# Operand tiles of the matrix products at different byte offsets within their buffers

## The chip, the cores and the metric

The kernel runs on one core of a Trainium2 chip, as one launch. The metric is the device time of that launch in microseconds (us). The kernel before was run three times: 972.31, 972.32 and 972.38 us, median 972.32 us. One further execution was taken by the hardware profiler.

## The reference

A trunk of two layers on 256 tokens of width 1024. Each layer is a half-step SwiGLU feed-forward block (FFN), a mixing block (two kinds of attention and a causal pooling, run side by side on one projected input), and a second half-step FFN. Every block starts with an RMS norm, and one more norm ends the trunk. All is float32.

```python
for l in range(2):
    x = x + 0.5 * swiglu(rmsnorm(x, ffn1_norm[l]), ffn1_w_gu[l], ffn1_w_down[l])
    x = x + hybrid_mixing(rmsnorm(x, mix_norm[l]), w_in[l], ..., w_out[l], pos)
    x = x + 0.5 * swiglu(rmsnorm(x, ffn2_norm[l]), ffn2_w_gu[l], ffn2_w_down[l])
return rmsnorm(x, final_norm)

def swiglu(h, w_gu, w_down):          # 1024 -> 2 x 2816 -> 1024
    gu = h @ w_gu
    g, u = gu[..., :D_FF], gu[..., D_FF:]
    return (jax.nn.silu(g) * u) @ w_down
```

## The kernel before

**Split products.** Nearly all products are made of three matmuls on the type float32r. Each operand is kept as a rounded part (high) and the rest that the rounding left (low), and high x high, high x low and low x high are added up in PSUM. The activations lie transposed, features on partitions and 256 tokens in a row. `mmw` (lines 229 to 231) loads a 128 x 128 piece of a weight as the stationary operand and streams 256 tokens past it. `mm3` (lines 222 to 224) has it the other way round: tokens are stationary and 288 to 512 columns of a weight stream.

**Tiles that the products read.**
- `hT` holds the normed input of a block, 8 chunks of 128 features, each with 256 high and 256 low values: 16 KB in each partition, one buffer for the whole kernel. Lines 403 and 410 write it; the gate and up products of an FFN (`gu_tile`) and the projections of the mixing block (`chunks`, `mix_head`) read it.
- `ph` and `pl` are the high and low parts of an FFN's inner activation, 1 KB in each partition, in 8 buffers each that are used in turn (`ptile`, line 524). The down product (`down`) reads them. In the mixing block the same buffers hold the inputs of the output projection.
- `hi` and `lo` are the high and low parts of a weight, 4 KB in each partition, in 8 buffers each. A weight arrives by DMA in `raw` (4 buffers, line 299), ScalarE rounds it to `hi` (line 320), and VectorE subtracts to get `lo` (line 335).

In the kernel before every one of these tiles starts at a multiple of 64 bytes. Counted within blocks of 128 bytes, `hT` starts at 64, and `ph`, `pl`, `hi` and `lo` start at 0. The norms are numbered: 0 and 3 feed the first FFN of a layer, 1 and 4 its mixing block, 2 and 5 its second FFN.

**Order.** An FFN goes over 22 chunks of 128 inner features. A chunk takes two gate/up tiles of 8 x 3 matmuls on `hT`, and, two chunks later, its down product, 8 x 3 matmuls on `ph` and `pl` into four PSUM banks. The kernel writes the order of the work on TensorE, ScalarE, VectorE and the DMA queue by hand, from an event simulation with fixed costs (`Issue`). These costs know nothing of addresses.

**Test products.** After all else, lines 1186 to 1195 issue 24 matmuls into a PSUM bank that nobody reads: 6 each on `hT` (512 columns), on a bfloat16 copy `pb` of part of `x`, on zeros `pz`, and on two halves of `hT`. GpSimd makes `pb` and `pz` at the start of the kernel (lines 1170 to 1174).

Of the kernel before, what the change touches and what calls it, by code (L numbers as in the profile page):

```python
# [10 lines left out]
F32 = mybir.dt.float32  # L11
F32R = mybir.dt.float32r
I32 = mybir.dt.int32
AF = mybir.ActivationFunctionType
ALU = mybir.AluOpType

P = 128
D = 1024
KC = 8
# [15 lines left out]
GUARD = 0.7  # L35
WB = 8
RB = 4

C_MASK, C_T, C_ROPE, C_INV, C_AB, C_END = 0, 256, 512, 640, 1152, 1164
V_B, V_PS, V_G, V_END = 0, 12, 16, 16 + L * 384  # L40
# [144 lines left out]
def trunk(ctx: ExitStack, tc: tile.TileContext, wpk, xin, gains, cst, vec, fst, out):  # L185
    nc = tc.nc
    V, A, T = nc.vector, nc.scalar, nc.tensor
    q = Issue()
    LAT = q.LAT

    cp = ctx.enter_context(tc.tile_pool(name="cp", bufs=1))
# [35 lines left out]
    def mmw(o, hi, lo, xh, xl, start, stop):  # L227

        T.matmul(o, lhsT=hi, rhs=xh, start=start, stop=False, skip_group_check=True)  # L229
        T.matmul(o, lhsT=hi, rhs=xl, start=False, stop=False, skip_group_check=True)  # L230
        T.matmul(o, lhsT=lo, rhs=xh, start=False, stop=stop, skip_group_check=True)  # L231
        return q.on("PE", 3 * 256 / 2185.0)
# [19 lines left out]
    vm = cp.tile([P, 2, 384], F32, name="vm")  # L252
    vf = cp.tile([P, 2, 384], F32, name="vf")
    up = [cp.tile([P, 272], F32, name=f"up{i}") for i in range(2)]
    hT = cp.tile([P, KC, 2, 256], F32R, name="hT")
    hTh, hTl = hT[:, :, 0, :], hT[:, :, 1, :]
    mhalf = cp.tile([P, 2], F32, name="mhalf")
    one = cp.tile([P, 1], F32, name="one")
    lf = [cp.tile([P, P], F32, name=f"lf{i}") for i in range(2)]
# [14 lines left out]
    def tbs(tb):  # L274
        return slice(tb * P, (tb + 1) * P)
# [32 lines left out]
    def hi_task():  # L308
        for u in range(NU):
            yield ev_slot[u], R_PREP  # L310
            rk = R_CHAIN + 0.1 * u if u < PARTS0 else R_PREP
            yield ev_raw[u], rk
            if u >= PARTS0:
                yield from calm("ACT", rk)
            w, r = units[u][3], raws[u]
            if units[u][0] == "poolw":
                h = wp.tile([P, 1024], F32, tag="hi", bufs=WB, name=f"hi{u}")
            else:
                h = wp.tile([P, 1024], F32R, tag="hi", bufs=WB, name=f"hi{u}")
            A.copy(h[:, :w], r[:, :w])  # L320
            his[u] = h
            ev_hi[u].set(act(w) + LAT)

    def lo_task():
        for u in range(NU):
            rk = R_CHAIN + 0.1 * u if u < PARTS0 else R_PREP
            yield ev_hi[u], rk, "DVE"
            if u >= PARTS0:
                yield from calm("DVE", rk)
            w, r, h = units[u][3], raws[u], his[u]  # L330
            if units[u][0] == "poolw":
                t = ev_hi[u].t
            else:
                lo = wp.tile([P, 1024], F32R, tag="lo", bufs=WB, name=f"lo{u}")
                V.tensor_tensor(out=lo[:, :w], in0=r[:, :w], in1=h[:, :w].bitcast(F32), op=ALU.subtract)  # L335
                los[u] = lo
                t = dve(w)
            ev_raw_free[u + RB].set(t + LAT)
            ev_w[u].set(t + LAT)

    uses = {}

# [26 lines left out]
    class N:  # L369


        def __init__(self, gi):
            self.gi = gi
            self.ev_h = [Ev() for _ in range(KC)]
            self.ss = sp.tile([P, 512], F32, tag="ss", bufs=1, name="ss")
            self.ev_ss = Ev()
            self.n = 0
            self.r, self.ev_r = None, Ev()
            self.R, self.Rh, self.ev_R = None, None, Ev()

    def resid(nm, i, acc, ev_acc, Rh):

        rk = R_CHAIN + 0.1 * i
        xs = x[:, 2 * i:2 * i + 2, :]
        yield ev_acc, rk, "DVE"
        if acc is not None:
            a = acc.rearrange("p (k t) -> p k t", k=2)
            if Rh is not None:
                d = sp.tile([P, 2, 256], F32, tag="dx", bufs=3, name="dx")
                V.tensor_tensor(out=d, in0=a, in1=bc(Rh, 2), op=ALU.mult)  # L390
                q.give(acc, dve(512) + LAT)
                V.tensor_tensor(out=xs, in0=xs, in1=d, op=ALU.add)  # L392
                t = dve(512)
            else:
                V.tensor_tensor(out=xs, in0=a, in1=xs, op=ALU.add)
                t = dve(512)
                q.give(acc, t + LAT)
            yield t + LAT, rk, "ACT"
        if nm is None:
            return  # L400
        for k in (2 * i, 2 * i + 1):
            g = fs[:, X_G + KC * nm.gi + k:X_G + KC * nm.gi + k + 1]
            A.activation(hTh[:, k, :], x[:, k, :], AF.Copy, scale=g)  # L403
            t = act(256)
            q.spawn(resid_lo(nm, k, g, t + LAT, rk))
        q.spawn(square(nm, i, xs, t + LAT))

    def resid_lo(nm, k, g, t, rk):
        yield t, rk, "DVE"
        V.scalar_tensor_tensor(out=hTl[:, k, :], in0=x[:, k, :], scalar=g, in1=hTh[:, k, :].bitcast(F32),  # L410
                               op0=ALU.mult, op1=ALU.subtract)
        nm.ev_h[k].set(dve(256) + LAT)

# [107 lines left out]
            nc.sync.dma_start(out[tb, :, c], h)  # L521


    def ptile(nm):
        return sp.tile([P, 256], F32R, tag=nm, bufs=8, name=nm)

    class F:

# [14 lines left out]
    def gu_tile(g, fc, j, k, b):  # L543
        n = parts(g.l, g.f, fc)
        m = KC // n
        u = g.W("gu", (fc, k // m))
        c = slice((k % m) * 256 + j * P, (k % m) * 256 + j * P + P)
        t = mmw(b[:, 0:256], his[u][:, c], los[u][:, c], hTh[:, k, :], hTl[:, k, :], k == 0, k == KC - 1)
        if k % m == m - 1:
            done(u, t, 2)  # L550
        return t
# [146 lines left out]
    def mix_head(g, tb):  # L698

        yield Banks(2), R_HEAD + 0.1 * tb  # L700
        bA, bB = q.take(2)
        for k in range(KC):
            yield g.nm.ev_h[k], R_HEAD + 0.1 * tb
            u = pos[("bq", g.l, k)]
            yield ev_w[u], R_HEAD + 0.1 * tb
            lh, ll, wh, wl = hTh[:, k, tbs(tb)], hTl[:, k, tbs(tb)], his[u], los[u]
            mm3(bA[:, 0:384], lh, ll, wh[:, 422:806], wl[:, 422:806], k == 0, k == KC - 1)
            t = mm3(bB[:, 0:422], lh, ll, wh[:, 0:422], wl[:, 0:422], k == 0, k == KC - 1)
            done(u, t, 2)
            yield t, R_HEAD + 0.1 * tb  # L710
        q.spawn(lowrank(g, tb, bA, t))
        q.spawn(gates(g, tb, bB, t))
        if tb == 1:
            q.spawn(chunks(g))
            q.spawn(qkv(g))
            q.spawn(decay(g))
            q.spawn(mix_out(g))
            for n, (kind, j) in enumerate(ATT_ORDER):
                q.spawn(attn(g, n, kind, j))
# [173 lines left out]
    def chunks(g):  # L893

        for kind in CHUNKS:
            yield Banks(1), R_MAIN
            b, = q.take(1)
            u = pos[(kind, g.l, 0)]
            yield ev_w[u], R_MAIN
            for k in range(KC):  # L900
                c = slice(k * P, (k + 1) * P)
                t = mmw(b[:, 0:256], his[u][:, c], los[u][:, c], hTh[:, k, :], hTl[:, k, :], k == 0, k == KC - 1)
                yield t, R_MAIN
            done(u, t)
            if kind[0] == "f":
                q.spawn(fox_evac(g, int(kind[3]), b, t))
            else:
                q.spawn(pool(g, int(kind[4]), b, t))
# [238 lines left out]
    with tc.manual_schedule(engines={mybir.EngineType.PE, mybir.EngineType.Activation, mybir.EngineType.DVE, mybir.EngineType.SP}):  # L1147
# [12 lines left out]
            nc.gpsimd.memset(up[i][:, 0:16], 0.0)  # L1160
            nc.gpsimd.memset(lf[i], 0.0)

        pb = cp.tile([P, 512], mybir.dt.bfloat16, name="pb")
        pz = cp.tile([P, 512], F32R, name="pz")

        def rest():
            yield 60.0, R_LATE
            dma(C_END / 2, lambda: nc.sync.dma_start(cs, cst))
            dma(V_END / 2, lambda: nc.sync.dma_start(ve, vec))
            nc.gpsimd.tensor_copy(pb, x[:, 0:2, :].rearrange("p k t -> p (k t)"))  # L1170
            zz = sp.tile([P, 256], F32, tag="pc", bufs=1, name="zz")
            nc.gpsimd.memset(zz, 0.0)
            nc.gpsimd.tensor_copy(pz[:, 0:256], zz)
            nc.gpsimd.tensor_copy(pz[:, 256:512], zz)

        q.spawn(rest())
        q.spawn(load_task())
# [4 lines left out]
            q.spawn(resid(n0, i, None, ev_x[i], None))  # L1182
        q.spawn(ffn(F(0, 0, n0), after_ffn1(0)))
        q.run()

        b, = q.take(1)
        w = hT[:, 0, 0, 0:P]
        for n in range(6):
            T.matmul(b, lhsT=hT[:, n, 0, 0:P], rhs=hT[:, n, :, :].rearrange("p a t -> p (a t)"), start=n == 0, stop=n == 5)
        for n in range(6):  # L1190
            T.matmul(b, lhsT=pb[:, 0:P], rhs=pb, start=n == 0, stop=n == 5)
        for n in range(6):
            T.matmul(b, lhsT=pz[:, 0:P], rhs=pz, start=n == 0, stop=n == 5)
        for n in range(6):
            T.matmul(b[:, 0:256], lhsT=hT[:, n, 0, 0:P], rhs=hT[:, n, :, 0:P], start=n == 0, stop=n == 5)

# [99 lines left out]
```

## Time and profile before

| | |
|---|---|
| median of 3 runs | 972.32 us |
| profiled execution | 973.32 us |
| its span, first to last instruction | 971.5 us |
| granted TensorE clock, mean | 0.996 of full speed |
| TensorE busy, matmul (PE) / weight load (PEld) | 952.3 / 927.7 us |
| VectorE (DVE) / ScalarE (ACT) / GpSimd (POOL) busy | 625.3 / 501.5 / 58.2 us |
| moved by DMA | 168.92 MB, mean 174 GB/s |

The matmul records overlap: one of 256 columns is recorded as some 280 ns long, while the next starts 113 to 119 ns after it. So busy time says nothing of TensorE's speed; the distance from start to start does, and it is read here from rows of the timeline.

### The profile page before, as it was taken

The numbers are of one execution on the slowest core, as the hardware profiler recorded it, in microseconds if no ns is written. First come the engines' busy times: TensorE is split into PE (matmuls) and PEld (weight loads), VectorE is DVE, ScalarE is ACT, GpSimd is POOL, SyncE is SP. The second block draws the span as 40 slices with busy tenths as digits, with TensorE's granted clock in tenths as the row PEclk, the third lists the DMA queues.
The fourth block names the chain that finished last, engine by engine and source line by source line (L and its number), as shares of the span: only waits on it lengthen the run. The fifth ranks groups of instructions, "written<-read, shape, count | busy, mean of one in ns | idle before, by whom it ended". The sixth has DMA issues, their size and how long they took to land.

```text
span 971.5 us, 18312 instructions
## 1 busy us (share of the span) xinstructions
PE 952.3 (98%) x7547; PEld 927.7 (95%) x7548; DVE 625.3 (64%) x1018; ACT 501.5 (52%) x797; POOL 58.2 (6%) x108
## 2 busy tenths in 40 slices
PE   8999999998999999999999999999999999999999
PEld 7999999997999999999999999999989999999997
DVE  6755555568996755555585555556599766555553
ACT  6544444456664644444464444445466665444442
POOL 1000000022220000000000000000504000000000
PEclk8999999999999999999999999999999999999999
DMA  7775555522453766655547655653423647566631
GB/s 247 233 265 189 185 186 191 161 84 93 136 192 103 263 199 195 188 187 188 177 137 232 194 181 189 182 180 104 149 91 117 211 134 263 189 196 194 191 115 44
DMA packets 48324, 168.92 MB, mean 174 GB/s; under 512 B 5360, under 2 KB 5744, under 8 KB 48240
## 3 DMA queue, kind: packets, MB, share of 16 engines
q1 hardware_dynamic: 48096, 167.66, 53.7%
q8 instruction: 59, 0.97, 0.4%
q14 instruction: 25, 0.20, 0.1%
q10 hardware_dynamic: 144, 0.09, 0.0%
HBM read 166.68 MB, written 1.05 MB: 173 GB/s over the span
## 4 chain that ended last, share of the span: by engine, by line
PE 85%; DVE 10%; POOL 2%; issue 1%; ACT 1%; DMA 1%; SPq 0%; DVEq 0%; POOLq 0%
PE bank L230 24%; PE bank L229 24%; PE bank L231 24%; PE bank L224 3%; PE bank L223 3%; PE bank L222 3%; DVE lo L335 3%; DVE fqk L944 1%; DVE pl L987 1%; PE bank L235 1%; POOL rsn L356 1%; PE bank L239 1%; DMA x<-xin 1%; DVE sm L998 1%; DVE e L1013 1%
## 5 line engine op out<-in xcount | busy, mean ns | idle before, releaser
L335 DVE TENSOR_TENSOR lo<-raw,hi 128x1024 fp32r<-128x1024 f32 (+3 forms) x320 | 382.7, 1204 | 187.4 <-ACT hi L320 184.6
L229 PE MATMUL bank<-hT,hi 128*128 128x256 f32 x1536 | 433.5, 282 | 0.0
L231 PE MATMUL bank<-hT,lo 128*128 128x256 f32 x1536 | 429.5, 280 | 0.6 <-DVE lo L335 0.4
L230 PE MATMUL bank<-hT,hi 128*128 128x256 f32 x1536 | 429.2, 279 | 0.0
L320 ACT CAST hi<-raw 128x1024 fp32r<-128x1024 f32 (+3 forms) x320 | 328.1, 1029 | 171.9 <-PE bank L230 111.6
L229 PEld LDWEIGHTS bank<-hT,hi 128*128 128x128 f32 x1536 | 291.7, 190 | 1.0
L231 PEld LDWEIGHTS bank<-hT,lo 128*128 128x128 f32 x1536 | 290.1, 189 | 1.3 <-DVE lo L335 1.1
L230 PEld LDWEIGHTS bank<-hT,hi 128*128 128x128 f32 x1536 | 289.6, 189 | 1.1
L229 PE MATMUL bank<-ph,hi 128*128 128x256 f32 x656 | 186.1, 284 | 0.0
L230 PE MATMUL bank<-pl,hi 128*128 128x256 f32 x656 | 184.8, 282 | 0.8 <-DVE pl L365 0.8
L231 PE MATMUL bank<-ph,lo 128*128 128x256 f32 x656 | 184.8, 282 | 0.0
L230 PEld LDWEIGHTS bank<-pl,hi 128*128 128x128 f32 x656 | 123.5, 188 | 1.1 <-DVE pl L365 1.0
L229 PEld LDWEIGHTS bank<-ph,hi 128*128 128x128 f32 x656 | 123.6, 188 | 0.1
L231 PEld LDWEIGHTS bank<-ph,lo 128*128 128x128 f32 x656 | 123.5, 188 | 0.0
L580 ACT ACTIVATE s<-s 128x256 f32<-128x256 f32 x88 | 36.4, 418 | 154.0 <-DVE s L576 153.9
L576 DVE TENSOR_TENSOR s<-bank,R 128x256 f32<-128x256 f32 x88 | 37.1, 424 | 43.2 <-PE bank L231 40.1
L365 DVE TENSOR_TENSOR pl<-p,ph 128x256 fp32r<-128x256 f32 x88 | 37.1, 424 | 38.0 <-ACT ph L362 38.0
L362 ACT CAST ph<-p 128x256 fp32r<-128x256 f32 x88 | 35.5, 406 | 25.3 <-DVE p L590 25.2
L356 POOL TENSOR_TENSOR rsn<-m,mhalf 128x2 f32<-128x2 f32 x6 | 9.3, 1551 | 647.2 <-DVE m L448 647.2
L590 DVE TENSOR_TENSOR p<-bank,s 128x256 f32<-128x256 f32 x88 | 36.6, 418 | 12.1 <-PE bank L231 9.6
L403 ACT ACTIVATE hT<-x,fs 128x256 fp32r<-128x256 f32 x48 | 21.8, 502 | 32.2 <-DVE x L392 18.3
L222 PE MATMUL bank<-lo,ph 128*128 128x512 f32 x88 | 34.7, 394 | 0.0
(155 smaller groups left out, 730.5 us busy)
## 6 DMA issues: line engine op xcount, KB each, us to landing
raw<-wpk SPq DMA_DIRECT2D x294, 512.0 KB, 4.1
raw<-wpk SPq DMA_DIRECT2D x16, 403.0 KB, 3.2
raw<-wpk SPq DMA_DIRECT2D x4, 288.0 KB, 3.5
x<-xin SPq DMA_DIRECT2D x4, 256.0 KB, 5.7
raw<-wpk SPq DMA_DIRECT2D x4, 256.0 KB, 5.7
out<-h SPq DMA_DIRECT2D x4, 256.0 KB, 2.1
raw<-wpk SPq DMA_DIRECT2D x2, 384.0 KB, 3.2
cs<-cst SPq DMA_DIRECT2D x1, 582.0 KB, 5.9
```

What stands on the lines that cost most here:

```text
L222: T.matmul(o, lhsT=lh, rhs=rl, start=start, stop=False)
L223: T.matmul(o, lhsT=ll, rhs=rh, start=False, stop=False)
L229: T.matmul(o, lhsT=hi, rhs=xh, start=start, stop=False, skip_group_check=True)
L230: T.matmul(o, lhsT=hi, rhs=xl, start=False, stop=False, skip_group_check=True)
L231: T.matmul(o, lhsT=lo, rhs=xh, start=False, stop=stop, skip_group_check=True)
L320: A.copy(h[:, :w], r[:, :w])
L335: V.tensor_tensor(out=lo[:, :w], in0=r[:, :w], in1=h[:, :w].bitcast(F32), op=ALU.subtract)
L362: A.copy(dh, src)
L365: V.tensor_tensor(out=dl, in0=src, in1=dh.bitcast(F32), op=ALU.subtract)
L576: V.tensor_tensor(out=s, in0=b[:, 0:256], in1=g.nm.R, op=ALU.mult)
L580: A.activation(s, s, AF.Silu)
L590: V.tensor_tensor(out=p, in0=b[:, 0:256], in1=g.s[fc], op=ALU.mult)
```

## The change

Each of the tiles gets some room in its buffer, and starts at an offset into it. The offset of `hT` goes by norm (64, 0, 32, 0, 0 and 16 bytes for the norms 0 to 5). Those of `ph` and `pl` go by turns, 0, 64, 32, 16, 96, 8, 80 and 4 bytes, in buffers whose pitch grows from 1024 to 1120 bytes. `hi` and `lo` get 0 bytes four times and 64 bytes four times in turn, and their pitch grows from 4096 to 4160 bytes. Counted within blocks of 128 bytes, the operands of the 6576 matmuls of 256 columns then start so:

| operand | before | after |
|---|---|---|
| `hT`, norms 0 to 5 | 64 | 0, 64, 96, 64, 64, 80 |
| `ph`, `pl` | 0 | spread over the block; in 1488 of 1968 matmuls at a multiple of 16 bytes, in 480 of them 4 or 8 bytes past one |
| `hi`, `lo` | 0 | 0 or 64 |
| `hT` less weight | 64 in all 4608 | 64 in 984, 0 in 1512, neither (16, 32, 80, 96) in 2112 |

The test products go, and with them `pb` and `pz`. No other instruction is added, removed or moved: the rows on each of the five engines are the same in the same order.

```diff
+OFF_X = [16, 0, 8, 0, 0, 4]
+OFF_P = [0, 16, 8, 4, 24, 2, 20, 1]
+OFF_W = [0, 0, 0, 0, 16, 16, 16, 16]
...
-    hT = cp.tile([P, KC, 2, 256], F32R, name="hT")
-    hTh, hTl = hT[:, :, 0, :], hT[:, :, 1, :]
+    hT = cp.tile([P, KC * 512 + 32], F32R, name="hT")
...
-                h = wp.tile([P, 1024], F32R, tag="hi", bufs=WB, name=f"hi{u}")
+                h = place(F32R, "hi", u)
...
-                lo = wp.tile([P, 1024], F32R, tag="lo", bufs=WB, name=f"lo{u}")
+                lo = place(F32R, "lo", u)
...
+    def place(dt, nm, u):
+        o = turn(nm, OFF_W)
+        return wp.tile([P, 1040], dt, tag=nm, bufs=WB, name=f"{nm}{u}")[:, o:o + 1024]
...
+            o = OFF_X[gi]
+            v = hT[:, o:o + KC * 512].rearrange("p (k s t) -> p k s t", k=KC, s=2)
+            self.hh, self.hl = v[:, :, 0, :], v[:, :, 1, :]
...
+    count = {"ph": 0, "pl": 0, "hi": 0, "lo": 0}
+
+    def turn(nm, offs):
+
+        count[nm] += 1
+        return offs[(count[nm] - 1) % len(offs)]
+
     def ptile(nm):
-        return sp.tile([P, 256], F32R, tag=nm, bufs=8, name=nm)
+        o = turn(nm, OFF_P)
+        return sp.tile([P, 280], F32R, tag=nm, bufs=8, name=nm)[:, o:o + 256]
...
-            nc.gpsimd.tensor_copy(pb, x[:, 0:2, :].rearrange("p k t -> p (k t)"))
-            zz = sp.tile([P, 256], F32, tag="pc", bufs=1, name="zz")
-            nc.gpsimd.memset(zz, 0.0)
-            nc.gpsimd.tensor_copy(pz[:, 0:256], zz)
-            nc.gpsimd.tensor_copy(pz[:, 256:512], zz)
...
-        b, = q.take(1)
-        w = hT[:, 0, 0, 0:P]
-        for n in range(6):
-            T.matmul(b, lhsT=hT[:, n, 0, 0:P], rhs=hT[:, n, :, :].rearrange("p a t -> p (a t)"), start=n == 0, stop=n == 5)
-        for n in range(6):
-            T.matmul(b, lhsT=pb[:, 0:P], rhs=pb, start=n == 0, stop=n == 5)
-        for n in range(6):
-            T.matmul(b, lhsT=pz[:, 0:P], rhs=pz, start=n == 0, stop=n == 5)
-        for n in range(6):
-            T.matmul(b[:, 0:256], lhsT=hT[:, n, 0, 0:P], rhs=hT[:, n, :, 0:P], start=n == 0, stop=n == 5)
```

## Rows read from the trace of the kernel before

**Rows 1.** The page: span, busy time by engine, granted clock in 40 slices.

```profile
span 971.5 us, 18312 instructions
PE 952.3 (98%) x7547; PEld 927.7 (95%) x7548; DVE 625.3 (64%) x1018; ACT 501.5 (52%) x797; POOL 58.2 (6%) x108
PEclk8999999999999999999999999999999999999999
```

**Rows 2.** The page: the chain that ended last, by engine.

```profile
PE 85%; DVE 10%; POOL 2%; issue 1%; ACT 1%; DMA 1%; SPq 0%; DVEq 0%; POOLq 0%
```

**Rows 3.** Groups by line: output and inputs, shapes, count | busy us, mean ns | idle before.

```profile
L229 PE MATMUL bank<-hT,hi 128*128 128x256 f32 x1536 | 433.5, 282 | 0.0
...
L229 PE MATMUL bank<-ph,hi 128*128 128x256 f32 x656 | 186.1, 284 | 0.0
...
L222 PE MATMUL bank<-lo,ph 128*128 128x512 f32 x88 | 34.7, 394 | 0.0
```

**Rows 4.** Busy time in 14 chunks of one FFN: us and instructions of each engine.

```profile
core 0: us, PE busy (x) PEld busy (x) DVE busy (x) ACT busy (x) POOL busy (x), PEclk, DMA share, GB/s
339.43:457.17 117.74, 117.74 (x1010) 117.74 (x1009) 66.80 (x85) 55.98 (x71) 0.00 (x0) 1.00 0.60 190
```

**Rows 5.** Timeline of TensorE: start us, us, line; 27 starts apart.

```profile
376.21 0.28 PE L229 MATMUL bank<-hT,hi 128*128 128x256 f32 x1
...
379.27 0.28 PE L229 MATMUL bank<-hT,hi 128*128 128x256 f32 x1
```

**Rows 6.** Timeline of TensorE in the chunk before; 33 starts apart.

```profile
367.06 0.28 PE L229 MATMUL bank<-hT,hi 128*128 128x256 f32 x1
...
370.94 0.28 PE L229 MATMUL bank<-hT,hi 128*128 128x256 f32 x1
```

**Rows 7.** Timeline of TensorE in a run of down products; 87 starts apart.

```profile
188.46 0.28 PE L229 MATMUL bank<-ph,hi 128*128 128x256 f32 x1
...
198.79 0.28 PE L229 MATMUL bank<-ph,hi 128*128 128x256 f32 x1
```

**Rows 8.** Timeline of TensorE in the mixing head; 3 starts apart.

```profile
200.97 0.34 PE L222 MATMUL bank<-lo,hT 128*128 128x384 f32 x1
...
201.51 0.35 PE L222 MATMUL bank<-lo,hT 128*128 128x422 f32 x1
```

**Rows 9.** Timeline of TensorE at a product of 384 columns in the mixing block; 6 starts apart.

```profile
227.59 0.34 PE L222 MATMUL bank<-lo,qkh 128*128 128x384 f32 x1
...
228.65 0.29 PE L222 MATMUL bank<-lo,qkh 128*128 128x288 f32 x1
```

**Rows 10.** Timeline of TensorE at the end: last product read by others, test products.

```profile
964.34 0.39 PE L224 MATMUL bank<-hi,ph 128*128 128x512 f32 x1
964.57 1.56 PE L1189 MATMUL bank<-hT 128*128 128x512 f32 x6
966.20 1.24 PE L1191 MATMUL bank<-pb 128*128 128x512 bf16 x5
...
968.66 0.87 PE L1195 MATMUL bank<-hT 128*128 128x256 f32 x6
```

**Rows 11.** Timeline of the DMA queue's engine (SP) at the end: the last two output transfers.

```profile
968.01 0.81 SPq L521 DMA_DIRECT2D out<-h  x2
```

**Rows 12.** Tile out: time from issue to landing, us, least, median, most.

```profile
DMA to landing us min/median/max: 2.0/2.1/2.3
```

**Rows 13.** Waits at the end: who waited for whom, us in total, times, longest.

```profile
SPq L1294 <- DMA out<-h: 1.6, 2, 1.1
```

**Rows 14.** Timeline of GpSimd at the start.

```profile
4.59 0.61 POOL L1170 CAST pb<-x 128x512 bf16<-128x512 f32 x1 [3.12 <-DMA x<-xin]
...
8.40 0.59 POOL L1174 CAST pz<-zz 128x256 fp32r<-128x256 f32 x1
16.49 1.61 POOL L356 TENSOR_TENSOR rsn<-m,mhalf 128x2 f32<-128x2 f32 x1 [7.49 <-DVE m L448]
```

**Rows 15.** Groups by line: the low part of a weight on VectorE.

```profile
L335 DVE TENSOR_TENSOR lo<-raw,hi 128x1024 fp32r<-128x1024 f32 (+3 forms) x320 | 382.7, 1204 | 187.4 <-ACT hi L320 184.6
```

More of the change, by code (lines that the diff above doesn't have):

```diff
@@ L316, in hi_task @@
             if units[u][0] == "poolw":
-                h = wp.tile([P, 1024], F32, tag="hi", bufs=WB, name=f"hi{u}")
+                h = place(F32, "hi", u)
             else:
-                h = wp.tile([P, 1024], F32R, tag="hi", bufs=WB, name=f"hi{u}")
+                h = place(F32R, "hi", u)
             A.copy(h[:, :w], r[:, :w])
@@ L402, in resid @@
             g = fs[:, X_G + KC * nm.gi + k:X_G + KC * nm.gi + k + 1]
-            A.activation(hTh[:, k, :], x[:, k, :], AF.Copy, scale=g)
+            A.activation(nm.hh[:, k, :], x[:, k, :], AF.Copy, scale=g)
             t = act(256)
@@ L409, in resid_lo @@
         yield t, rk, "DVE"
-        V.scalar_tensor_tensor(out=hTl[:, k, :], in0=x[:, k, :], scalar=g, in1=hTh[:, k, :].bitcast(F32),
+        V.scalar_tensor_tensor(out=nm.hl[:, k, :], in0=x[:, k, :], scalar=g, in1=nm.hh[:, k, :].bitcast(F32),
                                op0=ALU.mult, op1=ALU.subtract)
@@ L547, in gu_tile @@
         c = slice((k % m) * 256 + j * P, (k % m) * 256 + j * P + P)
-        t = mmw(b[:, 0:256], his[u][:, c], los[u][:, c], hTh[:, k, :], hTl[:, k, :], k == 0, k == KC - 1)
+        t = mmw(b[:, 0:256], his[u][:, c], los[u][:, c], g.nm.hh[:, k, :], g.nm.hl[:, k, :], k == 0, k == KC - 1)
         if k % m == m - 1:
@@ L705, in mix_head @@
             yield ev_w[u], R_HEAD + 0.1 * tb
-            lh, ll, wh, wl = hTh[:, k, tbs(tb)], hTl[:, k, tbs(tb)], his[u], los[u]
+            lh, ll, wh, wl = g.nm.hh[:, k, tbs(tb)], g.nm.hl[:, k, tbs(tb)], his[u], los[u]
             mm3(bA[:, 0:384], lh, ll, wh[:, 422:806], wl[:, 422:806], k == 0, k == KC - 1)
@@ L901, in chunks @@
                 c = slice(k * P, (k + 1) * P)
-                t = mmw(b[:, 0:256], his[u][:, c], los[u][:, c], hTh[:, k, :], hTl[:, k, :], k == 0, k == KC - 1)
+                t = mmw(b[:, 0:256], his[u][:, c], los[u][:, c], g.nm.hh[:, k, :], g.nm.hl[:, k, :], k == 0, k == KC - 1)
                 yield t, R_MAIN
@@ L1161, in trunk @@
             nc.gpsimd.memset(lf[i], 0.0)
-        pb = cp.tile([P, 512], mybir.dt.bfloat16, name="pb")
-        pz = cp.tile([P, 512], F32R, name="pz")
         def rest():
```

## The prediction

> **What bounds the kernel now.** I read the page first, then the chain, then the groups by line, then the timeline of TensorE at single matmuls. The page shows TensorE with a record open for 98% of the span at a full clock in all but the first slice, and DVE at 64% [rows 1]. The chain that ended last is TensorE for 85% and DVE for 10% [rows 2]. The groups say what it does: three lines of 1536 matmuls of 256 columns on hT, three of 656 on ph and pl, three of 88 with 512 columns, none with idle time before it [rows 3]. That is 4608, 1968 and 264 matmuls. So the time is a count of matmuls by their distance from start to start, and nothing that the change edits can matter much unless it alters that distance.
>
> The distance is where it gets interesting. Three stretches of the same instruction, 128 x 128 stationary and 256 columns moving:
> - hT, one stretch: 3.06 us over 27 starts, 113.3 ns [rows 5].
> - hT, the chunk before: 3.88 us over 33 starts, 117.6 ns [rows 6].
> - ph and pl: 10.33 us over 87 starts, 118.7 ns [rows 7].
>
> Over 14 chunks of one FFN, 117.74 us hold 672 matmuls on hT and 336 on ph (48 and 24 a chunk), TensorE never idle [rows 4]. With 336 x 118.7 ns = 39.9 us for ph, hT has 77.9 us, 115.9 ns each: about half of the time in the 113.3 cadence, half in the other. In the same stretch DVE is busy for 66.80 and ACT for 55.98 of 117.74 us [rows 4], so neither sets the pace there.
>
> Two things differ between hT and ph streams: hT starts at 64 and ph at 0 within blocks of 128 bytes, with the weights at 0; and the order in which they go through PSUM. That hT alone has the 113.3 cadence is what this change can break or spread. The test products show that the type matters too: six matmuls of 512 columns in float32r take (1.56 - 0.40)/5 = 232 ns apart, five in bfloat16 (1.24 - 0.38)/4 = 215 ns [rows 10] (the subtracted 0.40 and 0.38 are the length of a last record, 0.39 in the row above them). So a float32r stream loses some 17 ns that a bfloat16 stream doesn't, and this loss is the thing that could depend on where the operands lie.
>
> **The change, part by part.**
>
> *Test products at the end.* They run from 964.57 to 968.66 + 0.87 = 969.53 us [rows 10]. The last two output transfers are issued from 968.01 to 968.82 [rows 11] and land 2.1 us later [rows 12], near 970.9, and the end of the program waits for them, 1.6 us in two waits [rows 13]. The outputs don't read anything of the test products. So dropping them is worth 0; the cover is the output path of the last norm. Without that cover they would be worth 969.53 - 964.73 = 4.8 us, the end of the last useful matmul being 964.34 + 0.39.
>
> *pb and pz on GpSimd.* Over at 8.99 us, and the engine then idles for 7.49 us until the first norm [rows 14]. Worth 0. If that idle time were not there, 4 instructions of some 0.6 us would be 2 us at most.
>
> *Writes to shifted tiles.* The casts, subtractions and norms that write hi, lo, hT, ph and pl now write at other addresses. No row shows ACT or DVE writing at an odd start. In the FFNs they have over 40% of the time to spare [rows 4]. DVE's share of the chain is 10% [rows 2], and its longest group is lo, 1204 ns [rows 15], of which the two mixing blocks have 54. Bounds: 0, and 5% either way of 54 x 1204 ns, 3.3 us; I take 0, for weights stay at multiples of 64 bytes.
>
> *Reads by the products.* This is the term. I go by streams.
> - hT of norms 2 and 5, 2 x 1056 = 2112 matmuls. The start moves from 64 to 96 and 80; no weight keeps the distance of 64 bytes that all have now. No row shows such a stream. Bounds: 113.3 [rows 5] and 118.7 [rows 7]. I take 117.3, halfway from today's 115.9 to the ph stream: 2112 x 1.4 ns = +3.0 us.
> - hT of norms 0, 1, 3 and 4, 2 x 1056 + 384 = 2496 matmuls. By the program 984 of them keep the distance of 64 bytes to their weight and 1512 get one of 0, as ph has today; for these 1512 x 1.4 ns = +2.1 us. Bounds as before. The weight changes its buffer every 12 matmuls on the way through a tile, so a cadence that needs the distance is left and must be found again.
> - ph and pl, 1968 matmuls. 1488 start at a multiple of 16 bytes, 480 start 8 or 4 bytes past one. For a stream that is 8 bytes off there is one row: in the mixing head 384 columns start at 422 x 4 = 1688 bytes, and take 0.54/3 = 180 ns [rows 8]; 384 columns on a multiple of 64 take 1.06/6 = 177 ns [rows 9]. 3 ns in 384 columns is 2 ns in 256. 480 x 2 ns is +1.0 us. The others I leave where they are, 118.7; bounds are 113.3 (the best cadence spreads to them, 1488 x 5.4 ns = -8.0 us) and 2 ns more (+3 us).
> - 264 matmuls of 512 columns: the moving weights shift by 64 bytes in half of the cases. I take 0; by the spread of the 256-column rows (5.4 ns) the bounds are +-1.4 us.
>
> [...]
>
> Sum: 0 + 0 + 0 + 3.0 + 2.1 + 1.0 + 0 = +6.1 us. On the profiled execution that is 973.3 + 6.1 = 979.4, and its span 971.5 + 6.1 = 977.6. The median of the runs lies 1.0 below the profiled execution, so 972.3 + 6.1 = **978.4 us**. With half and twice of each term the forecast's own range is 975.5 to 984.5.
>
> **The rivals.**
>
> *The offsets change nothing.* The same hT, at the same addresses, runs at 113.3 and at 117.6 [rows 5, 6], so the cadence is chosen by history and not by address alone, and ph may differ from hT for its other way through PSUM. Against it: 87 starts on ph average 118.7 [rows 7], with two of three going on in the half of a PSUM bank where the last one wrote, as hT's do; a PSUM effect would have to sit in every third start alone. Time: 972.3.
>
> *The scatter frees the 117.6 cadence: faster.* If the 117.6 cadence is a collision of the two read streams that the present distances keep up, others may end it. All of hT at 113.3 would give 4608 x 2.6 ns = -12.0 us; ph at hT's average of 115.9 another 1968 x 2.8 = -5.5. It decides from the point where the gain in one stream outweighs the 6.1 us above; half of all of it, -8.8, gives 963.5, and a third, -5.8, gives 966.5, which I take. For it: the best cadence was met at a distance that is not 0, and the change makes many such distances. Against it: half of the hT stream has the best cadence already, and it can only be spread elsewhere.
>
> *The best cadence is lost everywhere.* All 4608 hT matmuls at 118.7: 4608 x 2.8 = +12.9, with 1.0 for the odd starts of ph +13.9: 986.2. For it: every other float32r stream here (ph, 384 and 512 columns) shows the larger loss. Against it: norms 1, 3 and 4 keep their start, and 984 matmuls the distance too.
>
> **How the numbers follow.** Forecast (slower by some 6 us) 43%, no effect 20%, faster 27%, best cadence lost 10%. A difference of 0.2%, 1.9 us, is about what can be told from no change. Slower by more: 43 + 10, less 1 for the forecast's low end, 52%. Within: the no-effect case and that 1, 21%. Faster: 27%. The range takes the rival at 966.5 as its low end and the lost cadence as its high end: 966 to 987; below it lies the stronger half of the faster case, above it odd starts that cost more than the row shows, together under 2 in 10.
>
> **What the profile after would show.** The starts on hT by FFN: the two second FFNs (norms 2 and 5) slower than the two first, no 113.3 stretch in them, the first FFNs with fewer 113.3 stretches than now. The starts on ph by turn: the same 118.7 in six of eight, 120 to 121 in those with 8 and 4 bytes. The end of the kernel after the last 512-column matmul unchanged at some 7 us. I would be wrong if the distances between starts don't depend on the offset at all (then the time stays within 1 us), if streams at 16, 32 or 48 bytes run at 113.3, or if DVE's lo shows another duration than 1204 ns.

## The result and the profile after

The changed kernel takes **980.67 us** (median of 4 runs, 979.90 to 981.05) against 972.32: a ratio of 1.0085, 95% interval 1.0067 to 1.0102, 8.4 us slower. The forecast was 978.4, the range 966 to 987. The profiled execution took 981.0 us.

The page after (span, busy time by engine, granted clock, chain by engine) answers to [rows 1, 2]:

```profile
span 979.2 us, 18260 instructions
PE 955.6 (98%) x7524; PEld 932.1 (95%) x7524; DVE 625.4 (64%) x1018; ACT 501.9 (51%) x797; POOL 56.0 (6%) x104
PEclk8999999999999999999999999999999999999999
PE 84%; DVE 11%; POOL 2%; issue 2%; ACT 1%; DMA 1%; SPq 0%; POOLq 0%; DVEq 0%
```

The span grew by 7.7 us. The clock is full where it was, DVE and ACT are as busy as they were, and 24 matmuls (the test products; 23 show) are gone. TensorE's busy time is up by 3.3 us though it has fewer matmuls; the table of busy times says no more than that. The four FFNs tell more, in the order of norms 0, 2, 3, 5. The first three rows go from an FFN's first product on hT to the first product on the next norm's hT, the last row from the first to the last product on hT: from:to, length, then busy time of PE, PEld, DVE, ACT, POOL, granted clock, DMA share, GB/s. Before:

```profile
6.93:218.92 211.99, 208.96 (x1702) 207.57 (x1700) 130.84 (x178) 107.81 (x154) 8.52 (x18) 0.98 0.60 194
296.28:489.26 192.98, 191.39 (x1636) 190.98 (x1635) 116.73 (x157) 94.48 (x130) 1.63 (x1) 1.00 0.57 181
489.26:695.92 206.66, 205.59 (x1702) 205.19 (x1700) 125.65 (x172) 102.27 (x144) 7.03 (x15) 1.00 0.55 174
772.99:953.31 180.32, 179.55 (x1339) 170.03 (x1338) 105.21 (x140) 88.35 (x120) 2.17 (x2) 1.00 0.54 174
```

After, and below them 14 chunks of norm 2's FFN, which answer to [rows 4]:

```profile
6.92:220.63 213.71, 210.70 (x1702) 209.29 (x1701) 130.76 (x178) 107.85 (x154) 6.90 (x15) 0.98 0.61 192
297.93:493.33 195.40, 193.82 (x1636) 193.41 (x1635) 116.65 (x157) 94.54 (x130) 1.63 (x1) 1.00 0.57 179
493.33:701.10 207.77, 206.76 (x1701) 206.31 (x1700) 125.75 (x172) 102.31 (x145) 7.00 (x15) 1.00 0.56 173
778.27:960.95 182.68, 181.93 (x1339) 172.15 (x1338) 105.30 (x140) 88.43 (x120) 2.18 (x2) 1.00 0.54 172
342.78:462.10 119.32, 119.32 (x1010) 119.32 (x1009) 66.68 (x85) 55.74 (x70) 0.00 (x0) 1.00 0.60 187
```

The FFNs are longer by 1.72, 2.42, 1.11 and 2.36 us, together 7.6 of the 7.7 us by which the span grew. Both second FFNs lose more than either first one. In the 14 chunks TensorE is never idle, the count of matmuls is the same, and 1.6 us are lost.

The starts show where. TensorE's timeline (start, length of the record, line) at the ends of four stretches of products on hT: 12 of norm 0 at distance 64 to their weight, 12 of norm 0 at distance 0, 48 of norm 2 at distance 32, 48 of norm 5 at distance 16. They answer to [rows 5, 6]:

```profile
64.53 0.28 PE L232 MATMUL bank<-hT,hi 128*128 128x256 f32 x1
...
65.77 0.28 PE L234 MATMUL bank<-hT,lo 128*128 128x256 f32 x1
...
38.98 0.28 PE L232 MATMUL bank<-hT,hi 128*128 128x256 f32 x1
...
40.30 0.28 PE L234 MATMUL bank<-hT,lo 128*128 128x256 f32 x1
...
376.83 0.28 PE L232 MATMUL bank<-hT,hi 128*128 128x256 f32 x1
...
382.42 0.28 PE L234 MATMUL bank<-hT,lo 128*128 128x256 f32 x1
...
857.28 0.28 PE L232 MATMUL bank<-hT,hi 128*128 128x256 f32 x1
...
862.63 0.28 PE L234 MATMUL bank<-hT,lo 128*128 128x256 f32 x1
```

That is 1.24/11 = 113 ns, 1.32/11 = 120, 5.59/47 = 118.9 and 5.35/47 = 113.8. These stretches are picked as clear cases; the averages below are closer together. Within one norm the cadence now changes with the weight's buffer, in norm 0 every 12 matmuls. From norm 2 on the turns of hi and lo are out of step in the program (one weight of each mixing block has no lo), so that the distance can also change between the three matmuls of one product.

Averages over all such starts (pairs over 160 ns apart left out), in ns; the distance of each product is that of its operands' addresses in the program:

| | before | after |
|---|---|---|
| hT, norms 0, 3 (first FFNs) | 115.6, 116.2 | 117.7, 117.6 |
| hT, norms 2, 5 (second FFNs) | 115.8, 115.4 | 118.4, 117.4 |
| hT, norms 1, 4 (mixing) | 116.7, 116.2 | 118.6, 117.7 |
| norm 0 after, distance 0 / 64 | | 118.7 / 116.8 |
| norm 2 after, distance 32 / 96 | | 118.4 / 118.5 |
| norm 5 after, distance 16 / 80 | | 116.7 / 119.2 |
| ph, pl: starts on 16 bytes (1475) | 118.7 | 118.0 |
| ph, pl: starts 4 or 8 past one (475) | 118.7 | 119.6 |

Summed over the starts, hT went from 525.7 to 535.0 us, ph and pl from 231.5 to 230.8, and the 512-column products from 60.9 to 60.8.

The end of the kernel, which answers to [rows 10 to 13]: last matmul, last four parts of the output, their time to landing, and the last wait.

```profile
971.95 0.40 PE L227 MATMUL bank<-hi,ph 128*128 128x512 f32 x1
```

```profile
970.79 5.64 SPq L530 DMA_DIRECT2D out<-h  x4
DMA to landing us min/median/max: 2.0/2.2/2.3
SPq L1292 <- DMA out<-h: 1.7, 2, 1.1
```

From the start of the last useful matmul to the end of the span it was 971.5 - 964.34 = 7.16 us, and is 979.2 - 971.95 = 7.25. The test products were worth nothing, and the end moved with that matmul, by 7.6 us. GpSimd's first norm and VectorE's lo answer to [rows 14, 15]; lo has the duration it had:

```profile
16.51 1.54 POOL L362 TENSOR_TENSOR rsn<-m,mhalf 128x2 f32<-128x2 f32 x1 [15.03 <-DVE m L457]
L337 DVE TENSOR_TENSOR lo<-raw,hi 128x1024 fp32r<-128x1024 f32 (+3 forms) x320 | 382.6, 1204 | 188.2 <-ACT hi L322 185.2
```

### The profile page after: what moved, and what is told of

Read it like the earlier page. It is cut to its first block, busy times and chain, and to the rows that moved or that the text cites. A ratio compares the mean times of both kernels' runs of the same rounds, so it can differ in the third digit from the quotient of the medians.

```text
span 979.2 us, 18260 instructions
## 1 busy us (share of the span) xinstructions
PE 955.6 (98%) x7524; PEld 932.1 (95%) x7524; DVE 625.4 (64%) x1018; ACT 501.9 (51%) x797; POOL 56.0 (6%) x104
## 4 chain that ended last, share of the span: by engine, by line
PE 84%; DVE 11%; POOL 2%; issue 2%; ACT 1%; DMA 1%; SPq 0%; POOLq 0%; DVEq 0%
PE bank L233 24%; PE bank L232 24%; PE bank L234 24%; PE bank L227 3%; PE bank L225 3%; PE bank L226 3%; DVE lo L337 3%; DVE fqk L961 1%; DVE pl L1004 1%; DVE sm L1015 1%; POOL rsn L362 1%; DVE e L1029 1%; DVE e L1030 1%; DMA x<-xin 1%; PE bank L238 1%
## 5 line engine op out<-in xcount | busy, mean ns | idle before, releaser
L337 DVE TENSOR_TENSOR lo<-raw,hi 128x1024 fp32r<-128x1024 f32 (+3 forms) x320 | 382.6, 1204 | 188.2 <-ACT hi L322 185.2
L322 ACT CAST hi<-raw 128x1024 fp32r<-128x1024 f32 (+3 forms) x320 | 328.1, 1029 | 176.0 <-PE bank L233 117.2
L227 PE MATMUL bank<-hi,ph 128*128 128x512 f32 x88 | 34.8, 395 | 0.0
```

The costliest lines, as they stand in the source:

```text
L227: T.matmul(o, lhsT=lh, rhs=rh, start=False, stop=stop)
```

## The experiments

Theory 1: the distance of the moving operand's start from the weight's, within 128 bytes, sets the cadence. Theory 2: the moving operand's own place does. Theory 3: neither does; hT is faster than ph for the order in which it goes through PSUM (the banks that the products add up in). Distances below are "moving less weight, within 128 bytes". The kernels are the kernel before without its test products, with the edit that is shown, but for three that are the changed kernel with other offsets; these are named. Averages by stream are each from one profiled execution. Most edits also widen the pitch of the buffers they shift, and no run did that alone; but the runs with the gates (ph and pl) at 64 and at 112 share one pitch and differ by 4.5 us, and in the first bench all pairs lie in the same two tiles.

**Test products alone.** The kernel before with the last two blocks of the change's diff, among them:

```diff
-        for n in range(6):
-            T.matmul(b, lhsT=pb[:, 0:P], rhs=pb, start=n == 0, stop=n == 5)
```

> Only the test products and the two tiles they read are dropped; all operand tiles start as before. Every theory: the outputs' transfers end the kernel as before, so 972.3 us (0 against before, at most 0.3), and the distances from start to start stay 115.9 ns on hT and 118.7 ns on ph. A rival that gives the test products a cost expects up to 4.8 us less, 967.5 us.

972.42 us, ratio 0.9999 (0.9990 to 1.0008). Worth nothing, so the whole 8.4 us come from the offsets, and what follows can be read against the kernel before.

**Gates at 64.**

```diff
-        return sp.tile([P, 256], F32R, tag=nm, bufs=8, name=nm)
+        return sp.tile([P, 288], F32R, tag=nm, bufs=8, name=nm)[:, 16:272]
```

> As e1, and ph and pl start at 64 in place of 0 within 128 bytes, so at the distance from their weights that hT has; nothing else moves. Theory 1 (the distance between the moving operand and the weight sets the cadence) and theory 2 (the moving operand's own start sets it) both expect ph to go from 118.7 to hT's 115.9 ns: 1968 x 2.8 ns = -5.5 us, 966.8 us, and down to 950 us if the 113.3 cadence, once met, holds through both streams. Theory 3 (the way through PSUM or the order of instructions makes ph slower, not its place) expects 118.7 ns and 972.3 us.

966.42 us, ratio 0.9939 (0.9921 to 0.9958). ph went from 118.7 to 116.9 ns with order and PSUM unchanged: theory 3, by which the place counts for nothing, falls. The hT streams, untouched, moved as well: 113.5 in norm 0, 117.2 in norm 2, 117.7 in norm 3. The profiled execution was the slowest of the four (969.68 us, the others 965.99 to 966.51), so the others probably had more of the good cadence than these averages. Two stretches of 48 on hT in norm 5, the same addresses within 128 bytes:

```profile
797.11 0.28 PE L229 MATMUL bank<-hT,hi 128*128 128x256 f32 x1
...
802.46 0.28 PE L231 MATMUL bank<-hT,lo 128*128 128x256 f32 x1
...
805.36 0.28 PE L229 MATMUL bank<-hT,hi 128*128 128x256 f32 x1
...
810.90 0.28 PE L231 MATMUL bank<-hT,lo 128*128 128x256 f32 x1
```

5.35/47 = 113.8 and 5.54/47 = 117.9. Either cadence, once entered, held to the end of these stretches. The kernel before shows the same: in norm 2 from 332.0 us on, the stretches of 48 on hT alternate strictly, 117.8, 113.9, 117.8, 113.9 and so on, 16 in a row. The "half and half" of the prediction is this alternation. The PSUM banks alternate with it, but they alone don't decide it: the last stretch of norm 0 in the kernel before has 96 products and by the program goes through both pairs of banks,

```profile
177.56 0.28 PE L229 MATMUL bank<-hT,hi 128*128 128x256 f32 x1
...
188.35 0.28 PE L231 MATMUL bank<-hT,lo 128*128 128x256 f32 x1
```

and keeps one cadence, 10.79/95 = 113.6, through banks that had 117.8 in the stretch before.

**All weights at 64.** hT keeps its place, ph too; the distances change places.

```diff
-                h = wp.tile([P, 1024], F32R, tag="hi", bufs=WB, name=f"hi{u}")
+                h = wp.tile([P, 1056], F32R, tag="hi", bufs=WB, name=f"hi{u}")[:, 16:16+1024]
...
-                lo = wp.tile([P, 1024], F32R, tag="lo", bufs=WB, name=f"lo{u}")
+                lo = wp.tile([P, 1056], F32R, tag="lo", bufs=WB, name=f"lo{u}")[:, 16:16+1024]
```

> As e1, and all weights hi and lo start at 64 in place of 0 within 128 bytes; hT stays at 64 and ph at 0. So the distance is 0 for hT and 64 for ph: the roles swap, while no moving operand of 256 columns has moved. Theory 1 expects hT at 118.7 ns (4608 x 2.8 = +12.9 us) and ph at 115.9 ns (-5.5 us): +7.4 us, 979.7 us. Theory 2 expects no change, 115.9 and 118.7 ns, 972.3 us. Theory 3 the same 972.3 us.

980.88 us, ratio 1.0078 (1.0063 to 1.0093). hT, which did not move, went to 118.8 to 119.1; ph, which did not move, went to 115.6. A run of 96 products on ph:

```profile
481.81 0.29 PE L229 MATMUL bank<-ph,hi 128*128 128x256 f32 x1
...
492.60 0.28 PE L231 MATMUL bank<-ph,lo 128*128 128x256 f32 x1
```

10.79/95 = 113.6, against the 118.7 of [rows 7], with the moving tiles at the same place within 128 bytes. Theory 2 falls as well.

**hT at 0**, so that no product of 256 columns has distance 64.

```diff
-    hT = cp.tile([P, KC, 2, 256], F32R, name="hT")
+    hT = cp.tile([P, KC * 512 + 32], F32R, name="hT")[:, 16:16 + KC * 512].rearrange("p (k s t) -> p k s t", k=KC, s=2)
```

> As e1, and hT starts at 0 in place of 64 within 128 bytes, so hT, ph and the weights all start alike. Theories 1 and 2 expect the 113.3 ns cadence to be gone and hT at ph's 118.7 ns: 4608 x 2.8 ns = +12.9 us, 985.2 us, which would be slower than the change itself. Theory 3 expects 115.9 ns on hT and 972.3 us.

986.47 us, ratio 1.0143 (1.0126 to 1.0159): hT at 118.7 to 118.9 in every norm. This is the "best cadence is lost everywhere" of the prediction. Its price, 985.2 without the 1.0 us for odd starts that this run doesn't have, is 1.3 us short.

**A bench.** Behind the kernel, 15 pairs of starts (weight, moving), three runs of 48 products each, with one narrow product of 144, 152 or 160 columns ahead of each run; nothing else is at work there but the output.

```diff
+        for wo, xo in BENCH:
+            for rep in range(3):
+                T.matmul(b[:, 0:144 + 8 * rep], lhsT=tw[:, 0:P], rhs=tx[:, 0:144 + 8 * rep], start=True, stop=True)
+                for n in range(48):
+                    T.matmul(b[:, 0:256], lhsT=tw[:, wo // 4:wo // 4 + P], rhs=tx[:, xo // 4:xo // 4 + 256], start=n == 0, stop=n == 47)
```

> As e1, with 15 pairs of starts measured one after the other behind the kernel's own work: for each pair 3 runs of 48 matmuls of 256 columns on two tiles of their own, the first matmul ahead of a run 144, 152 or 160 columns wide so that the runs begin at different moments; some 256 us more, into a PSUM bank that nobody reads. Starts within 128 bytes: weight 0 with moving 0, 16, 32, 48, 64, 80, 96, 112, 8, 4; then weight/moving 64/0, 64/64, 32/96, 32/32, 16/80. Theory 1 (distance alone): 64/0, 32/96 and 16/80 behave as 0/64 (113.3 or 117.6 ns), 64/64 and 32/32 as 0/0 (118.7 ns). Theory 2 (the moving operand's own start): 64/64 as 0/64, 64/0 as 0/0, and 32/32 as 0/32. A third reading, that what lies around the products (ACT, DVE, DMA) takes part, expects other numbers here than in the kernel, where these engines are at work. A starts 4 or 8 bytes off a multiple of 16 should cost 1 to 2 ns more than their neighbours.

TensorE's timeline, 48 products merged to a row: (0, 0), then the three runs of (0, 64), then (0, 112), (0, 4), (32, 32) and (16, 80), one of three each:

```profile
963.75 5.90 PE L1189 MATMUL bank<-tx,tw 128*128 128x256 f32 x48
...
1033.52 5.67 PE L1189 MATMUL bank<-tx,tw 128*128 128x256 f32 x48
...
1039.10 5.86 PE L1189 MATMUL bank<-tx,tw 128*128 128x256 f32 x48
...
1044.87 5.85 PE L1189 MATMUL bank<-tx,tw 128*128 128x256 f32 x48
...
1085.49 5.83 PE L1189 MATMUL bank<-tx,tw 128*128 128x256 f32 x48
...
1120.31 6.09 PE L1189 MATMUL bank<-tx,tw 128*128 128x256 f32 x48
...
1189.60 5.96 PE L1189 MATMUL bank<-tx,tw 128*128 128x256 f32 x48
...
1207.20 5.65 PE L1189 MATMUL bank<-tx,tw 128*128 128x256 f32 x48
```

Over the second half of each run the distance between starts is 118.6 ns at (0, 0) and (64, 64); 118.5 to 118.8 at 16 and 32; 118.3 at 96; 119.2 to 119.4 at 48 and 80; 117.0 at 112; 120.0 at 8; 120.0 to 122.7 at 4. In this bench both 113.3 and 117.8 occur at distance 64, and only there, with weights at 0, 64 and 32 (with the weight at 16, 113.3 alone). Of the five pairs that move the weight, four agree with theory 1, with no other engine at work. It misses one: (32, 32) gives 120.0 where its distance of 0 gives 118.6 elsewhere.

**The halves of the change.** The changed kernel, with hT and ph back in their places, or with the weights back at 0:

```diff
-OFF_X = [16, 0, 8, 0, 0, 4]
-OFF_P = [0, 16, 8, 4, 24, 2, 20, 1]
+OFF_X = [0, 0, 0, 0, 0, 0]
+OFF_P = [0, 0, 0, 0, 0, 0, 0, 0]
...
-OFF_W = [0, 0, 0, 0, 16, 16, 16, 16]
+OFF_W = [0, 0, 0, 0, 0, 0, 0, 0]
```

Weights moved alone:

> The change's offsets and pitch for the weights alone; hT and ph, pl start as before. By the program 2984 of 4608 hT matmuls have distance 0 and 1192 of 1968 on ph have distance 64. With e1 to e4's 118.8 ns at distance 0 and 115.6 at 64, theory 1 expects 2984 x 3.1 - 1192 x 3.1 ns = +5.6 us, 978 us, some more if the 113.3 cadence is lost when a weight changes its buffer in the middle of a tile. Theory 2 expects 972.3 us.

977.79 us, ratio 1.0052 (1.0035 to 1.0069). hT's starts cost 10.9 us more than with the test products dropped alone (524.2 to 535.1; 9 more pairs of starts are under 160 ns, so 9.8 us at an equal count), ph's 3.4 less (231.5 to 228.1).

hT, ph and pl moved alone:

> The change's offsets for hT, ph and pl alone; the weights all start at 0 as before. Theory 1, with the distances' cadences as read in the change's own trace (118.7 at 0, 118.5 at 96, 119.2 at 80, 118.2 on average for ph): norm 0 +3.3, norm 2 +3.0, norm 5 +3.7, norms 1, 3 and 4 0, ph and pl -1 us: +9 us, 981 us, more than the whole change, for there half of the weights moved along. Theory 2 expects the same order, +8 to +9.

984.22 us, ratio 1.0117 (1.0102 to 1.0132): 3 us more than expected. Norm 0 (distance 0) runs at 118.6, norm 2 (96) at 119.9, norm 5 (80) at 119.0, and gates at distance 4 at 122.6. Norm 3, which kept its distance of 64, sat at 117.8 for its whole FFN. The halves cost 5.4 and 11.8 us and the whole 8.3: they do not add up, as it must be if a difference of two places counts.

**A distance for each norm and turn.** The offsets of norms 0 to 5 give distances of 80, 32, 96, 112, 48 and 16 bytes, those of the gates 0 to 112 in steps of 16. The changed kernel, with weights at 0 and

```diff
-OFF_X = [16, 0, 8, 0, 0, 4]
-OFF_P = [0, 16, 8, 4, 24, 2, 20, 1]
+OFF_X = [4, 24, 8, 12, 28, 20]
+OFF_P = [0, 4, 8, 12, 16, 20, 24, 28]
```

> Weights at 0; the six norms' hT at 80, 32, 96, 112, 48 and 16 bytes, ph and pl in turn at 0, 16, 32, 48, 64, 80, 96 and 112 bytes within 128. It is to give the cadence by distance inside the kernel. Theory 1: a distance has one cadence, the same on hT and ph: 118.7 ns at 0, 113.3 or 117.6 at 64, by the change's trace 119.2 at 80, 118.5 at 96, about 116.3 at 112 and unknown at 16, 32 and 48; the time some 978 to 984 us. If instead only 64 is special, all others read 118.5 to 119.2 and the time is 984 us or more.

980.89 us (one run). hT by norm: 119.6, 118.4, 119.9, **114.1**, 119.2, 118.3. Norm 3, at 112, ran better than any norm of the kernel before (115.4 to 116.7), where the bench had 117.0 for this distance. Gates at 112 had 117.4: theory 1 in its strict form, one cadence for one distance, fails here.

**Everything at 112.**

```diff
-    hT = cp.tile([P, KC, 2, 256], F32R, name="hT")
+    hT = cp.tile([P, KC * 512 + 32], F32R, name="hT")[:, 12:12 + KC * 512].rearrange("p (k s t) -> p k s t", k=KC, s=2)
...
-        return sp.tile([P, 256], F32R, tag=nm, bufs=8, name=nm)
+        return sp.tile([P, 288], F32R, tag=nm, bufs=8, name=nm)[:, 28:284]
```

> Norm outputs and gates both lie 112 bytes behind the weights' place within 128 bytes (norm outputs 64 in the kernel before, gates 0). If the 114.1 ns that norm 3 showed at 112 in the run with a distance for each norm is what 112 gives in the kernel: hT 115.6 to 114.1 on 4,608 matmuls is -7 us, ph 118.7 to between 114.1 and 117.4 on 1,992 is -3 to -9: 956 to 963 us. If the 117.0 of the bench is the rule: hT +6.5, ph -3.4: about 975 us. If the time does not depend on the distance: 972.3 us.

**959.86 us**, ratio 0.9867 (0.9852 to 0.9882), the best of all and 12.5 us below the kernel before. Its four FFNs and the 14 chunks:

```profile
6.73:214.77 208.04, 204.72 (x1702) 203.10 (x1700) 130.59 (x178) 107.85 (x154) 6.91 (x15) 0.99 0.63 198
291.76:480.92 189.16, 187.56 (x1636) 187.16 (x1635) 116.67 (x157) 94.49 (x129) 1.63 (x1) 1.00 0.59 186
480.92:683.48 202.56, 201.45 (x1702) 200.96 (x1701) 125.66 (x172) 102.58 (x145) 7.01 (x15) 1.00 0.57 178
760.32:939.12 178.80, 178.05 (x1332) 168.21 (x1331) 105.34 (x140) 88.39 (x120) 2.18 (x2) 1.00 0.55 175
335.38:450.55 115.17, 115.17 (x1011) 115.17 (x1009) 66.67 (x85) 55.78 (x70) 0.00 (x0) 1.00 0.63 194
```

The 14 chunks take 115.17 us where they took 117.74 [rows 4] and, changed, 119.32. hT is at 113.8 to 114.6 in all four FFNs, ph at 115.9. Two stretches of 24 on ph in norm 2, both at distance 112:

```profile
423.21 0.28 PE L229 MATMUL bank<-ph,hi 128*128 128x256 f32 x1
...
425.82 0.28 PE L231 MATMUL bank<-ph,lo 128*128 128x256 f32 x1
...
439.54 0.28 PE L229 MATMUL bank<-ph,hi 128*128 128x256 f32 x1
...
442.23 0.28 PE L231 MATMUL bank<-ph,lo 128*128 128x256 f32 x1
```

2.61/23 = 113.5 and 2.69/23 = 117.0: distance 112 has two cadences as well, and the bench's 117.0 is one of them. On hT it is the good one that wins: in norms 0, 2 and 3, 58 of 59 stretches of 40 and more products run at 113.3 after their first 12, where 30 of 59 did in the kernel before. Since hT and ph differ at one and the same distance, the order of the products may still have a part; this was not tested.

**Two mixes**, from the edits above: hT at 112 (`12:`) with gates at 64 (`16:272`), and hT where it was, at 64, with gates at 112 (`28:284`):

> Norm outputs at distance 112, gates at 64. By the 114.1 of norm 3: hT -7 us, ph 118.7 to 116.9 as in the run with the gates at 64, -3.6: 961 to 962 us. By the bench's 117.0: hT +6.5, ph -3.6: about 975 us. It differs from the run with all at 112 in the gates alone: what separates the two is what 64 and 112 give on ph.

960.67 us, ratio 0.9876 (0.9861 to 0.9890): hT 114.1 to 114.4 in the FFNs, ph 115.8.

> Norm outputs at distance 64 as in the kernel before, gates at 112. ph at the 117.4 that 112 gave in the run with a distance for each turn: -2.6 us, and the norm outputs' streams keep their cadence across groups as they did with the gates at 64, up to -3.4 more: 966 to 970 us. If ph goes to 114.1 at a distance that stays 112: -9 us, 963 us. If only 64 lets the streams keep their cadence across the switch between hT and ph: 970 to 972 us.

961.92 us, ratio 0.9886 (0.9867 to 0.9905), below all three figures. hT, at the same 64 as in the kernel before, is at 113.6, 113.7 and 113.7 in norms 0, 2 and 3 (115.6 to 116.2 before) and ph at 116.9. The sum of hT's starts fell by 5.0 us (524.2 with the test products dropped alone, to 519.2), of ph's by 3.6 (231.5 to 227.9). (The first sum has 8 fewer pairs; at an equal count hT gained 6.0.) So the gates' offset gave more on hT, which it does not touch: what runs ahead of a stream has a part in its cadence. Norm 5 bears this out: no products of 256 columns on ph run between its stretches, and it stayed at 115.5 (115.4 before).

**A second bench**, to see why 112 differs between the bench and the kernel: the moving operand is the last norm's hT (at 64), the weight's start goes by the distance, one operand for all or alternating as in the kernel, six opening products of 136 to 156 columns.

```diff
...
+                for n in range(48):
+                    k, j = (n // 3) % 2 if kind == "k" else 0, n % 3 if kind != "s" else 0
+                    i = o + (2 * (j == 2) + k) * P
+                    T.matmul(b[:, 0:256], lhsT=tw[:, i:i + P], rhs=hT[:, k, int(j == 1), :], start=n == 0, stop=n == 47)
```

> After the kernel, seven sets of six runs of 48 products of 256 columns, each run opened by one product of 136 to 156 columns. The moving operand is the last norm's output, the stationary one a tile of its own, placed for the distance that is named. Set 1, distance 112, one weight and one moving tile for all 48, as in the first bench. Set 2, distance 112, the operands alternating as in the kernel (high x high, low x high, high x low). Set 3, the same over two chunks. Sets 4 and 5: the same two at distance 64. Set 6: distance 0 over two chunks. Set 7: distance 96 over two chunks. If one operand for all is what held the first bench at 117.0 ns: set 1 near 117, sets 2 and 3 near 113.3. If the moment of entry chooses at 112 as it does at 64: all three sets hold runs of both cadences. If the first bench's 117.0 is what the distance gives without other engines at work: all of sets 1 to 3 near 117. Sets 4 and 5: 113.3 and 117.8, run by run. Set 6: 118.6 or more in every run. Set 7: 118.3 in every run.

Set 1's first run, then the six runs of set 4 (distance 64):

```profile
972.51 5.96 PE L1190 MATMUL bank<-hT,tw 128*128 128x256 f32 x48
...
1078.11 5.66 PE L1190 MATMUL bank<-hT,tw 128*128 128x256 f32 x48
...
1083.67 5.67 PE L1190 MATMUL bank<-hT,tw 128*128 128x256 f32 x48
...
1089.25 5.86 PE L1190 MATMUL bank<-hT,tw 128*128 128x256 f32 x48
...
1095.02 5.65 PE L1190 MATMUL bank<-hT,tw 128*128 128x256 f32 x48
...
1100.57 5.86 PE L1190 MATMUL bank<-hT,tw 128*128 128x256 f32 x48
...
1106.34 5.85 PE L1190 MATMUL bank<-hT,tw 128*128 128x256 f32 x48
```

Sets 1 to 3 are at 120.0 in all 18 runs, which no theory expected; whether operands alternate makes no difference there. But their weights lie at 80, where the kernel has them at 0, so whether alternating operands matter at 112 with the weight at 0 was not tested. Set 6 (distance 0, both at 64) is at 118.5 to 118.8, set 7 (distance 96, weight at 96) at 120.0, where the first bench had 118.3 with the weight at 0. What these share with (32, 32) is a weight that is not on a multiple of 64: outside of distance 64 these pairs take 1.4 to 3 ns more. The change has its weights at 0 and 64 alone, so its own result is not touched; the bare rule "distance alone" is too simple. Sets 4 and 5 bear on the other point: openings of 136, 140 and 148 columns lead to 113.3, those of 144, 152 and 156 to 117.8, the same in both sets. So at distance 64 what came ahead decided the cadence, though not by its width alone: in the first bench an opening of 144 columns led to 113.3 at (0, 64) and to 117.8 at (32, 96).

## Why the prediction was right, and where its terms were off

The sign and the mechanism were right: the time went into the distance between starts, in hT's streams, in the FFNs, and nowhere else. 980.67 lies 2.3 us above the forecast and inside its own range (975.5 to 984.5; half of 6.1 gives 975.4). That it came so close is in part luck: the two hT terms were about half of what they should have been (5.1 against 9.3 us), and the ph term, which had the wrong sign, and the 0.7 us on hT that cost nothing made up for 2.4 us of it. By its steps:

- *Test products, pb and pz, shifted writes: 0 each.* Right. The run without them is within 0.1% of the kernel before, and VectorE's lo still takes 1204 ns.
- *hT of norms 2 and 5: +3.0 us.* Measured +4.9 (1056 x 2.6 + 1056 x 2.0 ns). The step that took "halfway" between 115.9 and 118.7 was too small for norm 2: at 32 and 96 nothing is left of the good cadence, 118.4 and 118.5.
- *hT of norms 0, 1, 3 and 4: +2.1 us.* Measured +4.4 (1056 x 2.1 + 1056 x 1.4 + 192 x 1.9 + 192 x 1.6 ns); the last two, 0.7 us, are in the mixing blocks and cost nothing there, for the time from one FFN's end to the next one's start stayed (296.28 - 218.92 = 77.36 us before, 297.93 - 220.63 = 77.30 after). The same half-way mark was used where 118.7, ph's own row, was at hand for distance 0: norm 0 has 118.7 there. The second part, that the good cadence must be found again every 12 matmuls, was seen but not priced: at distance 64 norm 0 went from 115.6 to 116.8. In norm 3 it cost nothing at that distance (116.1 before, 115.9 after).
- *ph and pl: +1.0 us.* Measured -0.7. The odd starts cost 0.9 ns each, not 2. By distance to the weight they fall apart: distance 4 has 122 to 124 ns, distance 68 has 118.5. The other starts got 0.8 ns better on average, 116.3 at distance 112, 118.1 at 64. The rival of a spread good cadence had this much in it.
- *512 columns: 0.* Right (-0.1).
- *The signs to look for.* "Second FFNs slower" is right by their time (2.42 and 2.36 us more, against 1.72 and 1.11), but not by the starts in norm 5: 117.4 ns, against 117.7 and 117.6 in norms 0 and 3. "The same 118.7" on ph in six of eight turns is not: by their start within 128 bytes these have 117.3 (at 112) to 119.0 (at 32); of the odd starts 72 has 120.1 and 4 has 119.1. "No 113.3 stretch in them" is wrong: norm 5 has stretches of 113.8 at 16 bytes. This is also one of the things that the prediction said would make it wrong; it stands beside 118.5 to 118.8 for the same distance in the bench and 118.3 in the run with a distance for each norm, so 16 bytes gives it only in some surroundings, and why stays open.

The first rival, no effect, falls with the runs that move one operand: for the same 256 columns these streams have 113.3 to 122.7 ns, and for float32r here the place of the one operand relative to the other does change the pace (ph 118.7 ns at distance 0 and 116.9 at 64, with hT and the weights in place). That the two read streams collide, as the rival "faster" had it, was not shown.

The rival "faster" was wrong for these offsets and right in kind: the offsets can give 12.5 us, but by a distance kept the same through each stream, not by a scatter. The change put distances of 0 to 112 side by side, most of them at 118 to 120, and broke up the one that half of the time had 113.3.

Open: what the good cadence is made of; why hT at 112 finds the 113.3 ns in the kernel and the first bench, with the weight at 0, stayed at 117.0 in its three runs; and why a weight at 32, 80 or 96 gave 120.0 at distances other than 64. The distance, the weight's own place and what ran just before all have a part; the distance alone is not a rule that gives the time.

## What to carry to other kernels

When TensorE has no idle time, look at the distance from start to start of equal matmuls: two values in one stream (113.3 and 117.6 ns here, both for 256 columns) were the sign that something other than the columns had a part in the pace. Here 2.7% of the kernel's time hung on it (959.9 to 986.5 us). Move one operand's tile against the other by 16 to 112 bytes for all products alike, measure in the kernel itself and not in a bench (distance 112 had 113.8 to 114.6 ns on hT in the kernel, and 117.0 in the first bench), and keep the one that wins. Don't scatter offsets: the scatters tried here (the change, each of its halves, a distance for each norm and turn) were all slower than the kernel before (977.8 to 984.2 us against 972.3); the two runs with one distance for hT and another for the gates were faster (960.7 and 961.9). And look at stretches, not only at averages: an offset that reaches the good cadence in every stretch is worth more than one that reaches it in every second one (58 of 59 here, against 30 of 59).

## What the hardware showed that was not expected

- One float32r stream of 256 columns at full clock (0.999 granted in both benches) took 113.3, 117.0, 117.8, 118.3 to 119.4, 120.0 or 122.7 ns a product, by the byte distance of its operands within 128, by the weight's own place (120.0 in one pair and four sets with the weight off the multiples of 64) and by what ran before. The worst is 4 bytes, up to 122.7 in the bench. A start 4 bytes past a multiple of 16 is no cost by itself: on ph in the change it has 118.5 ns at distance 68, and 122 to 124 at distance 4.
- At distance 64 two cadences sustained themselves, 113.3 and 117.8 ns; in the second bench an opening product 4 columns wider (144 in place of 140) was enough to change from one to the other. At distance 112 there were two as well, 113.5 and 117.0 on ph in the run with everything at 112.
